# Weight sums by GpSimd, and other shares of the work at a layer boundary

## The chip, the cores and the metric

The kernel runs on one core of a Trainium2 chip. The metric is the device time of one execution in microseconds (us); the median of the runs shown stands for a kernel. PE is TensorE, DVE is VectorE, ACT is ScalarE, POOL is GpSimd, SP is SyncE, whose queue issues most transfers.

## The reference

Two layers over 512 tokens of 1024 channels, in float32: an even layer (pooling mixer and gated mixer) and an odd one (dilated attention and short convolution). Cut to what the change touches:

```python
def even_layer(x, norm_g, w_in, pool_w, pool_scale, ws, bs, w_out):
    h = rmsnorm(x, norm_g)
    z = h @ w_in
    a, g_a, u, v, g_b = jnp.split(...)
    y_a = multiscale_pool(a, pool_w, pool_scale) * jax.nn.silu(g_a)
    y_b = chunk_spatial_gate(u, v, ws, bs) * jax.nn.silu(g_b)
    return x + jnp.concatenate([y_a, y_b], axis=-1) @ w_out

def odd_layer(x, norm_g, w_in, conv_w, w_out):
    h = rmsnorm(x, norm_g)
    z = h @ w_in
    ...
```

## The kernel before

Every product of the float32 data is made of three matmuls of high and low parts (`mm3`), so each tile of weights is loaded by SP as 128x2048 (1 MB), copied into its high part by ScalarE (L92, L226) and subtracted into its low part by VectorE (L93, L227). A `project` takes one such tile for 48 matmuls. The even layer runs, for each of four groups, `mixer_a` (projects a, ga) and `mixer_b` (u, gb), with the two halves of v ahead of groups 0 and 2. Three raw tiles (r...) are used in turn, so SP's queue can load about three projects ahead.

The output projection (`OutProj`, names eo and oo) and the odd layer's value products (`values`, names v0, w0, w1) each use seven products instead of eight, with sums and differences of quarters. Four of the seven factors on the weight side are sums of two or three blocks. There are 28 such sums of 1 MB: 8 for eo, 12 for the values (v), 8 for oo. Before, each is made in DRAM: SP copies one block into the sum's place (`copy_behind`, L190) and GpSimd's queue issues a DMA that adds another block into it (`add_behind`, L196). Block 6 is built on 7 and block 4 on 6, so some of the adding DMAs wait for another to land, and the wait stands in GpSimd's own order of instructions.

At the boundary between the layers the output projection ends in Z (product 4) and Y (product 3). VectorE adds the accumulated halves into the residual stream xt (L331, L336), and `normed` squares both halves of a tile of 128 tokens (L116, ScalarE), forms the reciprocal root with some 128x1 steps on VectorE (L118 to L123; ScalarE's Sqrt, L119), and scales two halves (L126, VectorE) into xb. `to_channels` transposes xb on TensorE (tx, L148), evicts it as hoh (L156, ScalarE) and hol (L157, VectorE) and once more as h32 (L159, ScalarE; the profile calls it h). The tiles of odd number, 1 and 3, come first; product 3 for the first half of the tiles runs ahead of tile 1's transposes, and for the second half behind them. Then v0Z (product 4 of the values) runs, then the transposes of tiles 0 and 2, then v0Y and v0X.

The order on each engine follows from a scheduler with priorities and is fixed in the program.

Of the kernel before, what the change touches and what calls it, by code (L numbers as in the profile page):

```python
# [30 lines left out]
def trunk(ctx, tc, x, w_even, w_eout, pool_w, ws_t, bs, par, g_even, w_v, w_odd, w_oout, g_odd, g_fin, cst, out):  # L31
# [74 lines left out]
        T.matmul(acc, al, bh, start=False, stop=last)  # L106


    def normed(tt, g, name, acc=None, then=None):
        o = sp.tile([P, D], F32, tag="xn", name=name, bufs=3)  # L110
        st = sp.tile([P, 64], F32, tag="st", name="st" + name, bufs=4)
        for h in range(2):
            xs = xt[:, tt, h * S:(h + 1) * S]
            if acc:
                V.tensor_add(xs, acc[h], xs)
            A.activation(o[:, h * S:(h + 1) * S], xs, AF.Square, accum_out=st[:, h:h + 1])  # L116
        ss, m, rt, u = (st[:, i:i + 1] for i in range(2, 6))
        V.tensor_add(ss, st[:, 0:1], st[:, 1:2])  # L118
        A.activation(rt, ss, AF.Sqrt, scale=1.0 / D, bias=eps[:, 0:1])  # L119
        V.tensor_scalar(m, ss, -0.5 / D, -0.5 * EPS, op0=ALU.mult, op1=ALU.add)  # L120
        V.reciprocal(rt, rt)
        V.scalar_tensor_tensor(u, rt, m, rt, op0=ALU.mult, op1=ALU.mult)
        V.scalar_tensor_tensor(u, u, 1.5, rt, op0=ALU.add, op1=ALU.mult)  # L123
        for h in range(2):
            at = slice(h * S, (h + 1) * S)
            V.scalar_tensor_tensor(o[:, at], xt[:, tt, at], u, g[:, at], op0=ALU.mult, op1=ALU.mult)  # L126
            if then:
                then(h, o[:, at])
        return o


# [41 lines left out]

    copies, adds = [], []

    def summed(src, name):
        n = src.shape[1]
        sums = {i: [dp.tile([P, CH], F32, tag=f"{name}{i}{q}", name=f"{name}{i}{q}") for q in range(n)] for i in range(4, 8)}  # L180
        b11, b12, b21, b22 = ([src[i, q] for q in range(n)] for i in range(4))
        for i, first, more in ((7, b12, b22), (5, b11, b12), (6, b11, sums[7]), (4, b21, sums[6])):
            copies.extend((sums[i][q], first[q]) for q in range(n))
            adds.extend((sums[i][q], more[q]) for q in range(n))
# [48 lines left out]


    class OutProj:
        def __init__(self, src, name, yy):
# [4 lines left out]
            self.src = summed(src, name)  # L241

        def form(self, view, n):
            f = ring(f"{self.name}f{n}").rearrange("p (w k t) -> p w k t", w=2, k=KT)
# [22 lines left out]
            self.f1 = self.form(b[0, 0], 1)  # L267
            V.tensor_sub(b[0, 0], b[0, 0], b[0, 1])

        def run(self, gains, half1, half0):  # L270
            with ExitStack() as stack:
                pool = stack.enter_context(tc.tile_pool(name=f"{self.name}w", bufs=1))
                self.chunks = Chunks(pool, 2)
                g = gain(pool, gains, f"g{self.name}")
                self.products(lambda t: half1(t, g), lambda t: half0(t, g))

        def products(self, half1, half0):
# [36 lines left out]
            f4 = self.form(b[1, 1], 4)  # L314
            for t in range(2):
                V.tensor_add(x(2 * t, 0), acc["X", t], x(2 * t, 0))

            both("Y", False, f6, w6)
            w4 = [self.parts(4, q) for q in range(2)]
# [23 lines left out]
    with ExitStack() as ec:  # L343
# [9 lines left out]
        def v_half(c):  # L353
# [17 lines left out]
            if c == 0:  # L371
                load(0, 4)
                to_channels(0, normed(0, ge, "xa0"), hth, htl)
                nc.sync.dma_start(xt[:, 1, :], x[P:2 * P, :])
                o = normed(1, ge, "xa1")
                load(1, 4)
                for tt in range(2, TT):
                    nc.sync.dma_start(xt[:, tt, :], x[tt * P:(tt + 1) * P, :])
                nc.sync.dma_start(pr, par)
                nc.sync.dma_start(wt, ws_t)  # L380
                nc.sync.dma_start(bsb.rearrange("p g t -> p (g t)"), bs.partition_broadcast(P))
                nc.sync.dma_start(cs[:, P:], cst[:, P:])
# [66 lines left out]
        def mixer_b(g, vb):  # L449
# [18 lines left out]
        even_out = OutProj(w_eout, "eo", yy)  # L468
        v_src = [summed(w_v[n:n + 1].rearrange("n b p c -> b n p c"), f"v{n}") for n in range(3)]

        for c in range(2):
            vb = v_half(c)
# [1 line left out]
                mixer_a(g)  # L474
                mixer_b(g, vb)

    o = {}
    odd = []

    def norm1(t, g):  # L480
        o[2 * t + 1] = normed(2 * t + 1, g, f"xb{2 * t + 1}")

    def norm0(t, g):
        if not odd:
            odd.extend(activations("ho"))
            odd.append(ring("h32", F32).rearrange("p (k t) -> p k t", k=KT))
        to_channels(2 * t + 1, o[2 * t + 1], *odd)
        o[2 * t] = normed(2 * t, g, f"xb{2 * t}")

    even_out.run(g_odd, norm1, norm0)  # L490
    hth, htl, h32 = odd


    slopes = [2.0 ** (-8.0 * (n + 1) / (SLOTS * N_DIL)) for n in range(SLOTS * N_DIL)]
    with ExitStack() as oc:
# [4 lines left out]
        def values():  # L500
# [17 lines left out]
            with ExitStack() as vc:  # L518
# [388 lines left out]
```

## Time and profile before

| | us |
|---|---|
| median of 3 runs | 1090.57 (1090.28 to 1090.58) |
| the profiled execution, its own time | 1091.0 |
| its span in the profile | 1089.2 |
| TensorE busy in the span | 1066.2 (98%) |
| VectorE, ScalarE, GpSimd busy | 573.8, 428.4, 191.8 |

The span runs from the first instruction to the last; 1.8 us of the execution's own time lie outside it. Busy time is a sum over the span, without instructions that only issue or wait.

### The profile page before, as it was taken

How to read it: one execution, taken by the hardware profiler on the slowest of the kernel's cores; microseconds unless marked ns; L12 is line 12 of the kernel's file. 1: busy time of each engine (PE TensorE's matmuls, PEld its weight loads, DVE VectorE, ACT ScalarE, POOL GpSimd, SP SyncE). 2: the span in 40 equal slices, each digit the busy share in tenths (PEclk: the TensorE clock that was granted, in tenths of full speed). 3: DMA queues.
4: the chain of work that ended last, by engine and by line, in shares of the span. 5: the costliest groups of instructions: out<-in, count | busy, mean ns of one | idle time of the engine just before them, and what ended most of it. 6: DMA issues, size and time to landing. Idle time of an engine off the chain costs nothing.

```text
span 1089.2 us, 12416 instructions
## 1 busy us (share of the span) xinstructions
PE 1066.2 (98%) x4928; PEld 891.4 (82%) x4928; DVE 573.8 (53%) x708; ACT 428.4 (39%) x583; POOL 191.8 (18%) x501
## 2 busy tenths in 40 slices
PE   6999999999998999999999999999999999999997
PEld 5888888888876888888888888888888888888885
DVE  6343324268969758824453534454444633434986
ACT  6322222326549554424252442434424322223644
POOL 0001030211050200003241442414134011010101
PEclk9999999999998999999999999999999999999999
DMA  9783599499999455663226263544131232223452
GB/s 335 304 326 119 193 265 286 113 245 282 324 272 250 155 193 190 257 270 133 78 78 155 78 155 97 136 116 118 75 113 43 97 116 100 94 102 131 155 193 77
DMA packets 36985, 185.69 MB, mean 170 GB/s; under 512 B 3328, under 2 KB 4480, under 8 KB 22272
## 3 DMA queue, kind: packets, MB, share of 16 engines
q1 hardware_dynamic: 21568, 154.50, 37.9%
q0 software_dynamic: 14784, 29.36, 15.0%
q10 hardware_dynamic: 576, 1.05, 0.3%
q8 instruction: 38, 0.62, 0.2%
q14 instruction: 19, 0.16, 0.0%
HBM read 182.80 MB, written 60.82 MB: 224 GB/s over the span
## 4 chain that ended last, share of the span: by engine, by line
PE 96%; DVE 2%; ACT 1%; DMA 1%; issue 0%; SPq 0%; DVEq 0%
PE q L106 8%; PE q L104 8%; PE q L105 8%; PE v L104 1%; PE v L106 1%; PE v L105 1%; PE gc L106 1%; PE gc L105 1%; PE u L105 1%; PE dx L104 1%; PE dx L106 1%; PE db L106 1%; PE dc L104 1%; PE gc L104 1%; PE dc L106 1%; PE gd L106 1%
## 5 line engine op out<-in xcount | busy, mean ns | idle before, releaser
L104 PE MATMUL q<-hoh,hq 128*128 128x512 f32 x384 | 151.1, 393 | 0.0
L106 PE MATMUL q<-hoh,lq 128*128 128x512 f32 x384 | 149.7, 390 | 0.0
L105 PE MATMUL q<-hol,hq 128*128 128x512 f32 x384 | 149.5, 389 | 0.0
L106 PEld LDWEIGHTS q<-hoh,lq 128*128 128x128 f32 x384 | 72.1, 188 | 15.2
L105 PEld LDWEIGHTS q<-hol,hq 128*128 128x128 f32 x384 | 72.2, 188 | 14.6
L104 PEld LDWEIGHTS q<-hoh,hq 128*128 128x128 f32 x384 | 72.1, 188 | 14.4
L92 ACT ACTIVATE hq<-rq 128x2048 fp32r<-128x2048 f32 x24 | 46.0, 1916 | 86.4 <-PE q L105 72.4
L93 DVE TENSOR_TENSOR lq<-rq,hq 128x2048 fp32r<-128x2048 f32 x24 | 54.8, 2285 | 16.1 <-ACT hq L92 16.1
L658 DVE COPY qk<-q 128x512 f32<-128x512 f32 x24 | 16.6, 690 | 88.3 <-PE q L106 88.3
L660 ACT ACTIVATE qk<-q 128x512 f32<-128x512 f32 x24 | 14.3, 596 | 72.5 <-PE q L106 72.4
L700 ACT ACTIVATE yo<-yo,nm 128x128 f32<-128x128 f32 (+1 forms) x96 | 39.9, 417 | 5.1 <-DVE nm L692 4.7
L464 POOL TENSOR_TENSOR ye<-ye,sggb 128x1024 f32<-128x1024 f32 x3 | 12.0, 4014 | 162.1 <-ACT sggb L409 162.1
L227 DVE TENSOR_TENSOR lw<-rw,hw 128x2048 fp32r<-128x2048 f32 x14 | 32.4, 2319 | 15.3 <-ACT hw L226 15.3
L227 DVE TENSOR_TENSOR loo<-roo,hoo 128x2048 fp32r<-128x2048 f32 x14 | 34.0, 2435 | 11.4 <-ACT hoo L226 11.4
L226 ACT ACTIVATE heo<-reo 128x2048 fp32r<-128x2048 f32 x14 | 26.7, 1916 | 29.5 <-issue 9.2
L226 ACT ACTIVATE hoo<-roo 128x2048 fp32r<-128x2048 f32 x14 | 26.7, 1915 | 28.6 <-DMA roo<-oo 7.8
L227 DVE TENSOR_TENSOR leo<-reo,heo 128x2048 fp32r<-128x2048 f32 x14 | 33.0, 2365 | 9.2 <-ACT heo L226 9.2
L761 POOL TENSOR_TENSOR yo<-yo,at 128x512 f32<-128x512 f32 x8 | 12.3, 1544 | 140.2 <-DVE at L759 140.2
L226 ACT ACTIVATE hw<-rw 128x2048 fp32r<-128x2048 f32 x14 | 26.7, 1910 | 20.1 <-PE w0Y L538 6.0
L724 DVE TENSOR_SCALAR yo<-yo,ff 128x128 f32<-128x128 f32 (+1 forms) x96 | 23.3, 299 | 17.1 <-POOL ff L722 14.2
L790 POOL TENSOR_TENSOR yo<-cv,dc 128x512 f32<-128x512 f32 x6 | 13.2, 2205 | 92.3 <-ACT dc L789 92.3
L759 DVE TENSOR_TENSOR at<-oa,at 128x512 f32<-128x512 f32 x8 | 5.5, 691 | 40.4 <-ACT at L758 40.4
(394 smaller groups left out, 2841.2 us busy)
## 6 DMA issues: line engine op xcount, KB each, us to landing
rq<-in_w_odd SPq DMA_DIRECT2D x24, 1024.0 KB, 4.8
reo<-eo SPq DMA_DIRECT2D x8, 1024.0 KB, 8.0
rw<-v SPq DMA_DIRECT2D x8, 1024.0 KB, 4.8
roo<-oo SPq DMA_DIRECT2D x8, 1024.0 KB, 4.7
reo<-in_w_eout SPq DMA_DIRECT2D x6, 1024.0 KB, 7.7
v<-in_w_v POOLq DMA_DIRECT2D x6, 1024.0 KB, 20.1
v<-v POOLq DMA_DIRECT2D x6, 1024.0 KB, 13.5
rw<-in_w_v SPq DMA_DIRECT2D x6, 1024.0 KB, 4.8
```

Source lines behind the costliest of these rows:

```text
L92: A.activation(hi[:, at], raw[:, at], AF.Copy)
L93: V.tensor_sub(lo[:, at], raw[:, at], hi[:, at].bitcast(F32))
L104: T.matmul(acc, ah, bh, start=first, stop=False)
L105: T.matmul(acc, ah, bl, start=False, stop=False)
L106: T.matmul(acc, al, bh, start=False, stop=last)
L226: A.activation(hi, raw, AF.Copy)
L227: marks["lo"] = V.tensor_sub(lo, raw, hi.bitcast(F32))
L658: V.tensor_copy(to, by)
L660: A.activation(to, by, AF.Copy, scale=HEAD ** -0.5)
L700: A.activation(v, v, AF.Exp, bias=nm[:, g, n:n + 1], accum_out=ls[:, g, n:n + 1])
L724: V.tensor_scalar_mul(v, v, ff[:, g, n:n + 1])
L790: (V if c == 3 else G).tensor_mul(y[4 + c][:, j, :], cv[j][:, 0:S], dc[j][:, 0:S])
```

## The change

Three things change. First, the sums for eo and for the first two of the three value sets (16 MB of the 28) are made on the chip: 16 steps, each of which loads four blocks as one 128x4x512 tile into one half of a ring tile named sums (L232), lets GpSimd do four adds of 128x512 in place (L234), and stores the four results as one transfer (L225). The load of a step and the store of the step before it are issued by SP behind the weight load of a project. The four sums of the third value set are made as before, by a copy and an adding DMA, and these DMAs now stand between the adds. Second, in the first three groups the product of mf and the gate goes from GpSimd to VectorE. Third, at the boundary `normed` is split. The half of a tile that is finished first is squared early (`square`), GpSimd multiplies that half by the gain (L140) and makes two 128x1 steps, and `normed_rest` squares the late half, scales the early half on ScalarE (L147) and the late one on VectorE (L148). For tiles 0 and 2 h32 is made by GpSimd from hoh and hol, and GpSimd makes the first difference of h32 (L638).

```diff
+    def square(pool, tt, h):
+        st = sp.tile([P, 64], F32, tag="st", name=f"stxb{tt}", bufs=4)
+        junk = pool.tile([P, S], F32, tag="sq", name=f"sq{tt}", bufs=2)
+        A.activation(junk, xt[:, tt, h * S:(h + 1) * S], AF.Square, accum_out=st[:, 0:1])
+        G.tensor_scalar(st[:, 1:2], st[:, 0:1], 1.0 / D, EPS, op0=ALU.mult, op1=ALU.add)
+        G.tensor_scalar(st[:, 2:3], st[:, 0:1], -0.5 / D, -0.5 * EPS, op0=ALU.mult, op1=ALU.add)
+        return st
+
+    def normed_rest(tt, h, st, g, name):
...
+        G.tensor_mul(o[:, other], xt[:, tt, other], g[:, other])
+        A.activation(o[:, late], xt[:, tt, late], AF.Square, accum_out=s1)
+        A.activation(rt, s1, AF.Sqrt, scale=1.0 / D, bias=e0)
+        V.tensor_scalar(m, s1, -0.5 / D, m0, op0=ALU.mult, op1=ALU.add)
...
+        A.activation(o[:, other], o[:, other], AF.Copy, scale=u)
+        V.scalar_tensor_tensor(o[:, late], xt[:, tt, late], u, g[:, late], op0=ALU.mult, op1=ALU.mult)
...
             A.activation(dh, bv, AF.Copy)
+            if h32 is not None and tt % 2:
+                A.activation(d32, bv, AF.Copy)
             V.tensor_sub(dl, bv, dh.bitcast(F32))
-            if h32 is not None:
-                A.activation(d32, bv, AF.Copy)
+            if h32 is not None and tt % 2 == 0:
+                G.tensor_add(d32, dh.bitcast(F32), dl.bitcast(F32))
...
+    def sum_behind(load):
+        with tc.issue_after(load.ins):
+            if under_way:
+                dst, t = under_way.pop()
+                nc.sync.dma_start(dst, t)
...
+            src, dst = steps.pop(0)
+            t = pool_sums[0][:, len(steps) % 2]
+            nc.sync.dma_start(t, src)
+        for a, b, c in ((3, 3, 1), (1, 1, 0), (0, 0, 3), (2, 2, 0)):
+            marks["sum"] = G.tensor_add(t[:, a], t[:, b], t[:, c])
+        under_way.append((dst, t))
...
         wh, wl = weights(src, name)
-        copy_behind(marks["load"], 2 if name[0] in "ua" else 1)
+        if name != "a0":
+            sum_behind(marks["load"])
+        copy_behind(marks["load"], 1)
...
-                self.last = G.tensor_sub(x(2 * t + 1, 0), x(2 * t + 1, 0), v[:, t, :])
-            add_behind(self.last, 4)
+                G.tensor_sub(x(2 * t + 1, 0), x(2 * t + 1, 0), v[:, t, :])
+                if early:
+                    early(2 * t + 1, 1)
...
-                add_behind(G.tensor_mul(mf, mf, sg), (0, 4, 12)[g])
+                V.tensor_mul(mf, mf, sg)
+                if g == 2:
+                    add_behind(marks["sum"], 4)
...
-                        V.tensor_sub(hb[0, 1], hb[0, 1], hb[1, 1])
+                        G.tensor_sub(hb[0, 1], hb[0, 1], hb[1, 1])
```

The order on GpSimd from the start of the even layer to the output projection, before (L464 is the product with the gate, L196 an adding DMA, xt the residual stream):

```order
L464 TENSOR_TENSOR ye<-ye,sggb_873 128x1024
L196 DMA eo_94<-in_w_eout 512x512
L196 DMA eo_95<-in_w_eout 512x512
L196 DMA eo_90<-in_w_eout 512x512
L196 DMA eo_91<-in_w_eout 512x512
L464 TENSOR_TENSOR ye<-ye,sggb_1285 128x1024
L196 DMA eo_92<-eo_94 512x512
L196 DMA eo_93<-eo_95 512x512
L196 DMA eo_88<-eo_92 512x512
L196 DMA eo_89<-eo_93 512x512
```

And after (L234 is an add of a step, L246 an adding DMA):

```order
L234 TENSOR_TENSOR sums<-sums 128x512 x52
L246 DMA v_95<-in_w_v 512x512
L246 DMA v_93<-in_w_v 512x512
L246 DMA v_94<-v_95 512x512
L246 DMA v_92<-v_94 512x512
L234 TENSOR_TENSOR sums<-sums 128x512 x12
L355 TENSOR_TENSOR xt<-xt,eos_1796 128x512 x2
```

The adding DMAs for eo and for two value sets are gone; the four that are left stand after the adds of the thirteenth step, ahead of the adds of steps 14 to 16.

The order on SP at the end of the even layer, before (L190 is a copy, ra to rgb the weights of a project, reo those of the output projection):

```order
L91 DMA ra_1366<-in_w_even 128x2048
L190 DMA v_106<-in_w_v 16x16384
L190 DMA v_104<-in_w_v 16x16384
L91 DMA rga_1443<-in_w_even 128x2048
L419 DMA pwr_1358<-in_pool_w 128x2x256
L91 DMA ru_1513<-in_w_even 128x2048
L91 DMA rgb_1592<-in_w_even 128x2048
```

And after (L232 loads a step, L225 stores one; the store in the second row is step 13's, the one ahead of ru is step 14's):

```order
L91 DMA ra_1406<-in_w_even 128x2048
L225 DMA v_91<-sums 128x4x512
L232 DMA sums<-in_w_v 128x4x512
L91 DMA rga_1487<-in_w_even 128x2048
L232 DMA sums<-in_w_v 128x4x512
L475 DMA pwr_1398<-in_pool_w 128x2x256
L225 DMA v_91<-sums 128x4x512
L91 DMA ru_1563<-in_w_even 128x2048
L225 DMA v_91<-sums 128x4x512
L232 DMA sums<-in_w_v 128x4x512
L91 DMA rgb_1648<-in_w_even 128x2048
L225 DMA v_91<-sums 128x4x512
```

The load of ru now stands behind the store of step 14, which needs the fourteenth group of GpSimd's adds.

The order on VectorE at the boundary from the addition of tile 0's late half, before (stxb and xb belong to the norm, lv to the values' weights, hol to the evictions of tile 1 and then tile 3):

```order
L126 SCALAR_TENSOR_TENSOR xb_2093<-xt,stxb_2094,geo 128x512 x2
L157 TENSOR_TENSOR hol<-tx_2133,hoh 128x512
L157 TENSOR_TENSOR hol<-tx_2141,hoh 128x512
L118 TENSOR_TENSOR stxb_2150<-stxb_2150 128x1
L120 TENSOR_SCALAR stxb_2150<-stxb_2150 128x1
L121 RECIPROCAL stxb_2150<-stxb_2150 128x1
L122 SCALAR_TENSOR_TENSOR stxb_2150<-stxb_2150 128x1
L123 SCALAR_TENSOR_TENSOR stxb_2150<-stxb_2150 128x1
L126 SCALAR_TENSOR_TENSOR xb_2149<-xt,stxb_2150,geo 128x512 x2
L227 TENSOR_TENSOR lv_2232<-rv_2229,hv_2231 128x2048
```

And after:

```order
L391 TENSOR_TENSOR xt<-eoY_1869,xt 128x512
L143 TENSOR_SCALAR stxb_2001<-stxb_2001 128x1
L144 RECIPROCAL stxb_2001<-stxb_2001 128x1
L145 SCALAR_TENSOR_TENSOR stxb_2001<-stxb_2001 128x1
L146 SCALAR_TENSOR_TENSOR stxb_2001<-stxb_2001 128x1
L148 SCALAR_TENSOR_TENSOR xb_2218<-xt,stxb_2001,geo 128x512
L279 TENSOR_TENSOR lv_2297<-rv_2294,hv_2296 128x2048
L179 TENSOR_TENSOR hol<-tx_2202,hoh 128x512
L179 TENSOR_TENSOR hol<-tx_2210,hoh 128x512
L391 TENSOR_TENSOR xt<-eoY_1882,xt 128x512
```

Tile 1's two evictions into hol now stand behind tile 0's norm and behind a weight difference lv; before they stood ahead of both.

## Rows read from the trace of the kernel before

**Rows 1.** Windows, whole program: length, busy per engine, granted clock, transfer share, GB/s.

```profile
12.00:300.00 288.00, 287.59 (x1304) 238.25 (x1304) 147.85 (x137) 104.59 (x105) 28.66 (x22) 1.00 0.82 255
300.00:355.00 55.00, 48.58 (x210) 39.52 (x209) 44.02 (x55) 38.94 (x50) 15.28 (x11) 0.94 0.95 255
355.00:1050.00 695.00, 695.00 (x3268) 584.92 (x3267) 352.51 (x462) 259.25 (x389) 142.59 (x460) 1.00 0.40 131
```

**Rows 2.** Waits of PE at the boundary, 300 to 360: total us, times, longest us.

```profile
PE tx L148 <- DVE xb L126: 4.3, 2, 2.2
PE v0Z L536 <- ACT hoh L156: 0.9, 1, 0.9
PE v0Y L538 <- DVE vf L232: 0.8, 1, 0.8
PE v0Z L538 <- DVE hol L157: 0.4, 1, 0.4
```

**Rows 3.** A window at the boundary, columns as in rows 1.

```profile
348.00:350.00 2.00, 1.85 (x4) 1.49 (x5) 2.00 (x4) 2.00 (x3) 0.00 (x0) 0.50 1.04 349
```

**Rows 4.** PE's timeline: start, duration, instruction, [idle before, releaser].

```profile
227.91 0.48 PE L104 MATMUL u<-heh,hu 128*128 128x512 f32 x1
...
325.71 0.55 PE L148 MATMUL tx<-cs,xb 128*128 128x128 f32 x3 [2.21 <-DVE xb L126]
...
354.65 0.40 PE L536 MATMUL v0X<-hv,hoh 128*128 128x512 f32 x1
```

**Rows 5.** GpSimd's timeline, columns as in rows 4.

```profile
89.06 4.01 POOL L464 TENSOR_TENSOR ye<-ye,sggb 128x1024 f32<-128x1024 f32 x1 [69.32 <-ACT sggb L409]
...
310.82 1.30 POOL L325 TENSOR_TENSOR xt<-xt,eov 128x512 f32<-128x512 f32 x1
312.06 2.01 POOL L196 DMA_DIRECT2D v<-in_w_v  x2
...
338.70 1.04 POOL L196 DMA_DIRECT2D v<-v  x1 [13.63 <-DMA v<-v]
```

**Rows 6.** VectorE's timeline, columns as in rows 4.

```profile
88.53 2.29 DVE L93 TENSOR_TENSOR lga<-rga,hga 128x2048 fp32r<-128x2048 f32 x1 [9.75 <-ACT hga L92]
...
310.95 3.31 DVE L227 TENSOR_TENSOR leo<-reo,heo 128x2048 fp32r<-128x2048 f32 x1 [3.17 <-ACT heo L226]
...
318.37 2.28 DVE L227 TENSOR_TENSOR leo<-reo,heo 128x2048 fp32r<-128x2048 f32 x1
...
329.20 2.02 DVE L157 TENSOR_TENSOR hol<-tx,hoh 128x512 fp32r<-128x512 f32 x2
```

**Rows 7.** A window of the even layer, columns as in rows 1.

```profile
30.00:250.00 220.00, 219.98 (x1005) 183.11 (x1004) 89.97 (x80) 62.46 (x59) 24.57 (x15) 1.00 0.73 229
```

**Rows 8.** SyncE's queue: start of each issue, duration.

```profile
19.66 0.52 SPq L91 DMA_DIRECT2D ru<-in_w_even  x1
...
150.05 0.33 SPq L91 DMA_DIRECT2D rgb<-in_w_even  x1
...
182.45 0.34 SPq L91 DMA_DIRECT2D ru<-in_w_even  x1
```

**Rows 9.** Transfers: KB each, median us to landing; first 12 to 60, then 160 to 210.

```profile
ru<-in_w_even SPq DMA_DIRECT2D x1, 1024.0 KB, 16.3
...
rga<-in_w_even SPq DMA_DIRECT2D x1, 1024.0 KB, 9.5
...
rgb<-in_w_even SPq DMA_DIRECT2D x1, 1024.0 KB, 4.7
```

**Rows 10.** ScalarE's timeline, columns as in rows 4.

```profile
215.35 1.92 ACT L92 ACTIVATE hu<-ru 128x2048 fp32r<-128x2048 f32 x1 [4.66 <-PE a L105]
...
314.21 1.92 ACT L226 ACTIVATE hv<-rv 128x2048 fp32r<-128x2048 f32 x1 [3.29 <-DMA rv<-v]
...
322.64 1.28 ACT L119 ACT_TABLE_LOAD   x1
...
326.63 2.00 ACT L156 ACTIVATE hoh<-tx 128x512 fp32r<-128x512 f32 x2
```

More of the change, by code (lines that the diff above doesn't have):

```diff
@@ L106, in mm3, with normed @@
         T.matmul(acc, al, bh, start=False, stop=last)
-    def normed(tt, g, name, acc=None, then=None):
+    def normed(tt, g, name):
         o = sp.tile([P, D], F32, tag="xn", name=name, bufs=3)
@@ L126, in normed @@
             V.scalar_tensor_tensor(o[:, at], xt[:, tt, at], u, g[:, at], op0=ALU.mult, op1=ALU.mult)
-            if then:
-                then(h, o[:, at])
+        return o
+    def square(pool, tt, h):
[6 more added lines that the diff above has]
+    def normed_rest(tt, h, st, g, name):
+        o = sp.tile([P, D], F32, tag="xn", name=name, bufs=3)
+        s1, e0, m0, rt, m, u = (st[:, i:i + 1] for i in (3, 1, 2, 4, 5, 6))
+        late, other = (slice(n * S, (n + 1) * S) for n in (h, 1 - h))
+        G.tensor_mul(o[:, other], xt[:, tt, other], g[:, other])
+        A.activation(o[:, late], xt[:, tt, late], AF.Square, accum_out=s1)
+        A.activation(rt, s1, AF.Sqrt, scale=1.0 / D, bias=e0)
+        V.tensor_scalar(m, s1, -0.5 / D, m0, op0=ALU.mult, op1=ALU.add)
+        V.reciprocal(rt, rt)
+        V.scalar_tensor_tensor(u, rt, m, rt, op0=ALU.mult, op1=ALU.mult)
+        V.scalar_tensor_tensor(u, u, 1.5, rt, op0=ALU.add, op1=ALU.mult)
+        A.activation(o[:, other], o[:, other], AF.Copy, scale=u)
+        V.scalar_tensor_tensor(o[:, late], xt[:, tt, late], u, g[:, late], op0=ALU.mult, op1=ALU.mult)
         return o
@@ L172, in tick, with summed @@
                 item[1]()
-    copies, adds = [], []
-    def summed(src, name):
+    copies, adds, steps, under_way = [], [], [], []
+    pool_sums = [None]
+    def summed(src, name, on_chip):
         n = src.shape[1]
-        sums = {i: [dp.tile([P, CH], F32, tag=f"{name}{i}{q}", name=f"{name}{i}{q}") for q in range(n)] for i in range(4, 8)}
         b11, b12, b21, b22 = ([src[i, q] for q in range(n)] for i in range(4))
-        for i, first, more in ((7, b12, b22), (5, b11, b12), (6, b11, sums[7]), (4, b21, sums[6])):
-            copies.extend((sums[i][q], first[q]) for q in range(n))
-            adds.extend((sums[i][q], more[q]) for q in range(n))
-        return {1: b11, 2: b21, 3: b22, **sums}
+        if on_chip:
+            both = [dp.tile([4, P, CH], F32, tag=f"{name}{q}", name=f"{name}{q}") for q in range(n)]
+            for q in range(n):
+                for i in range(4):
+                    at = slice(i * S, (i + 1) * S)
+                    steps.append((src[:, q, :, at].rearrange("b p c -> p b c"), both[q][:, :, at].rearrange("b p c -> p b c")))
+            sums = {m: [both[q][i] for q in range(n)] for i, m in enumerate((6, 5, 4, 7))}
+        else:
+            sums = {i: [dp.tile([P, CH], F32, tag=f"{name}{i}{q}", name=f"{name}{i}{q}") for q in range(n)]
+                    for i in range(4, 8)}
+            for i, first, more in ((7, b12, b22), (5, b11, b12), (6, b11, sums[7]), (4, b21, sums[6])):
+                copies.extend((sums[i][q], first[q]) for q in range(n))
+                adds.extend((sums[i][q], more[q]) for q in range(n))
+        return {1: b11, 2: b21, 3: b22, **sums}
+    def sum_behind(load):
[3 more added lines that the diff above has]
+                nc.sync.dma_start(dst, t)
+            if not steps:
+                return
+            if pool_sums[0] is None:
+                pool_sums[0] = ring("sums", F32).rearrange("p (s b c) -> p s b c", s=2, b=4)
+            src, dst = steps.pop(0)
[4 more added lines that the diff above has]
+        under_way.append((dst, t))
     def copy_behind(load, n):
@@ L240, in __init__ @@
             self.bank = {}
-            self.src = summed(src, name)
+            self.src = summed(src, name, on_chip)
         def form(self, view, n):
@@ L268, in prepare, with run @@
             V.tensor_sub(b[0, 0], b[0, 0], b[0, 1])
-        def run(self, gains, half1, half0):
+        def run(self, gains, half1, half0, early=None):
             with ExitStack() as stack:
@@ L274, in run, with products @@
                 g = gain(pool, gains, f"g{self.name}")
-                self.products(lambda t: half1(t, g), lambda t: half0(t, g))
-        def products(self, half1, half0):
+                self.products(lambda t: half1(t, g), lambda t: half0(t, g), early and (lambda tt, h: early(pool, tt, h)))
+        def products(self, half1, half0, early):
             b, nm, acc = self.block, self.name, self.bank
@@ L316, in products @@
                 V.tensor_add(x(2 * t, 0), acc["X", t], x(2 * t, 0))
+                if early:
+                    early(2 * t, 0)
             both("Y", False, f6, w6)
@@ L324, in products @@
                 G.tensor_add(x(2 * t + 1, 1), x(2 * t + 1, 1), v[:, t, :])
-                self.last = G.tensor_sub(x(2 * t + 1, 0), x(2 * t + 1, 0), v[:, t, :])
-            add_behind(self.last, 4)
+                G.tensor_sub(x(2 * t + 1, 0), x(2 * t + 1, 0), v[:, t, :])
+                if early:
+                    early(2 * t + 1, 1)
             both("Z", False, f4, w4, True)
@@ L398, in v_half @@
                     load(kh)
+                    sum_behind(marks["load"])
                     for t in range(TT):
@@ L463, in mixer_b @@
                 sg = gate(w_even[7 + 4 * g], f"gb{g}")
-                add_behind(G.tensor_mul(mf, mf, sg), (0, 4, 12)[g])
+                V.tensor_mul(mf, mf, sg)
+                if g == 2:
+                    add_behind(marks["sum"], 4)
             else:
                 sg = gate(w_even[7 + 4 * g], f"gb{g}", lambda j, t: V.tensor_mul(mf[:, j, :], mf[:, j, :], t))
-        even_out = OutProj(w_eout, "eo", yy)
-        v_src = [summed(w_v[n:n + 1].rearrange("n b p c -> b n p c"), f"v{n}") for n in range(3)]
+        even_out = OutProj(w_eout, "eo", yy, True)
+        v_src = [summed(w_v[n:n + 1].rearrange("n b p c -> b n p c"), f"v{n}", n < 2) for n in range(3)]
         for c in range(2):
@@ L475, in trunk, with early @@
                 mixer_b(g, vb)
-    o = {}
+    o, st = {}, {}
     odd = []
+    def early(pool, tt, h):
+        st[tt] = square(pool, tt, h)
     def norm1(t, g):
-        o[2 * t + 1] = normed(2 * t + 1, g, f"xb{2 * t + 1}")
+        o[2 * t + 1] = normed_rest(2 * t + 1, 0, st[2 * t + 1], g, f"xb{2 * t + 1}")
     def norm0(t, g):
@@ L487, in norm0 @@
         to_channels(2 * t + 1, o[2 * t + 1], *odd)
-        o[2 * t] = normed(2 * t, g, f"xb{2 * t}")
-    even_out.run(g_odd, norm1, norm0)
+        o[2 * t] = normed_rest(2 * t, 1, st[2 * t], g, f"xb{2 * t}")
+    even_out.run(g_odd, norm1, norm0, early)
     hth, htl, h32 = odd
```

6 lines of the change are left out of this document (2 added, 4 removed).

## The prediction

> **What bounds the kernel now.** I read the windows over the whole program first: TensorE works 287.59 of 288 us in the even layer and all of 355 to 1050; between them, at the layer boundary, it works 48.58 of 55 us and at a mean granted clock of 0.94 [rows 1]. So the kernel is bound by TensorE, and only the boundary has something to give: 6.4 us of idle time, and 48.58 x 0.06 = 2.9 us from the clock, 9.3 us in all. The waits of TensorE say where: twice for xb (4.3 us in all, the longest 2.2), 0.9 for hoh, 0.4 for hol, 0.8 for the form vf [rows 2]. One of the windows behind them stands at 0.50, the lower of the two levels (1.2 of 2.4 GHz), with TensorE busy before and behind [rows 3]. Even layer and odd layer can only lose. A change of under 0.2% (2.2 us) can't be told from none by a measurement of this kernel.
>
> **The change, part by part: the sums.** Of the 28 copies with their adding DMAs 16 go. TensorE waits for no transfer in the rows [rows 2], so taking them away gives nothing; what covers them is that each sum is due long after it is made. What comes in is a chain with a due time. A step is a load, four adds on GpSimd, a store, and SP issues the store ahead of the next project's weights, so SP stops where GpSimd is late. I follow it to the one place where it matters, the load of the last u weights (ru), behind the store of step 14.
>
> TensorE takes these weights at 227.91 [rows 4]. A split needs ScalarE 1.92 us [rows 10] and VectorE 2.29 [rows 6], together 4.2. A transfer of 1 MB lands after 4.7 alone and 9.5 among others [rows 9]; I take 8, since each project now has a load and a store beside its weights. So ru must leave SP by 227.9 - 4.2 - 8 = 215.7; before, it left at 182.45 [rows 8], 33 us earlier.
>
> When does step 14's store leave? A GpSimd add of 128x512 takes 1.30 us when alone [rows 5], so four take 5.2. But the two engines get in each other's way: a GpSimd product of 128x1024 took 4.01 us from 89.06, where VectorE's 128x2048 difference ran from 88.53 to 90.82; without these first 1.76 us it would be 2.25 [rows 5, 6]. And VectorE's difference of 310.95 took 3.31 instead of 2.28 beside a GpSimd op that ended at 312.12 [rows 5, 6]. VectorE is busy 89.97 of 220 us of the even layer, 41% [rows 7], a part of it with an input from PSUM, where I see no such delay. So four adds cost from 5.2 to 5.2 / 0.59 = 8.8; I take 7. The Trainium skill ("SBUF — State Buffer", "Who interferes with whom") says that a VectorE instruction with two SBUF inputs and a GpSimd instruction that reads SBUF exclude each other for a whole instruction; the two pairs of rows agree.
>
> Two steps share the ring tile and overlap: store, load (with its landing), four adds, four adds. A pair costs a landing of 4.7 to 9.5 [rows 9], two groups of adds (10.4 to 17.6) and some 0.6 of issues: 15.7 to 27.7, and I take 8 + 14 + 0.6 = 22.6. The first step's load stands just ahead of ru, which leaves at 19.66 [rows 8] and lands 16.3 later among the first loads [rows 9]; so it lands at about 32 and its adds end near 38. Six pairs on, the thirteenth step ends at 38 + 136 = 174. It can't end before its load does, which stands behind gb's weights at 150.05 [rows 8]: 150.4 + 4.7 + 5.2 = 160. With the high ends it ends at 38 + 166 = 204.
>
> Behind the thirteenth step GpSimd issues the four adding DMAs that are left. The third waits for the first to land, the fourth for the third. The same four took from 312.06 to 338.70 + 1.04, 27.7 us, before [rows 5]; two lone landings would be some 23. Then the adds of step 14 (7), the store, and ru. Middle: 174 + 27.7 + 7 + 0.6 = 209.3 against 215.7, so TensorE doesn't wait, with 6 us to spare. Cost nil; the cover is those 6 us, and past them each us is lost on TensorE. Best: 160 + 23 + 5.2 + 0.6 = 189. Worst: 204 + 34 + 8.8 + 0.6 = 247, some 32 us late, if everything is slow at once.
>
> The Trainium skill ("GPSIMD Engine Reference", "Engine selection") puts elementwise work on VectorE, since GpSimd takes about twice as long; its table has 4.5 us for 2048 columns, so an estimate by that page is 1.1 us for 512. By that, the four adds would take 4.5 us and the middle would have a few us more to spare; the row, 1.30, goes.
>
> The product with the gate, on VectorE three times, is no cost: GpSimd's 4.01 us become some 1.2 of an engine that is 41% busy [rows 5, 7].
>
> **The boundary.** Squares taken early take 0.63 us of ScalarE and one half of VectorE's scaling (0.7 of 1.4) out of the chain from the last addition to xb. I count the chain anew by the order of each engine.
>
> First stall. Before, GpSimd ended its two pairs of xt updates at 312.12 [rows 5], ahead of most of VectorE's difference [rows 6]. After, a gain product (1.30) and two small steps stand between the pairs, so the second pair begins after VectorE's difference has begun, waits for its end (312.8) and ends its first half at 314.2. ScalarE's early square of tile 3 waits for that, and stands ahead of hv, which moves from 314.21 [rows 10] to 314.9; VectorE's lv and leo then meet GpSimd's other products (1.3 each). The last leo, which began at 318.37 and took 2.28 [rows 6], ends at about 322.6 instead of 320.65. TensorE, which needs it at 320.3, waits 2.2. From there the chain is an addition 0.7, a square 0.8, the table load 1.28 [rows 10], Sqrt 0.3, four small steps 0.8, the scaling 0.75: the transposes of tile 1 begin at 326.9 instead of 325.71 [rows 4]: +1.2.
>
> Second stall. 32 matmuls and the transposes further, at about 334.8, TensorE needs tile 1's hol. VectorE has it behind lv, which waits for ScalarE's hv, which stands behind four evictions (from 328.4, two took 2.00 at 326.63 [rows 10], with an overlap: 0.92 each), a square 0.8 and a Sqrt 0.3: hv from 333.2 to 335.1, lv to 337.4, and two hol of 1.0 each [rows 6] to 339.4. TensorE waits 4.6 where it waited 0.9 + 0.4 [rows 2]: +3.3. Before, hol ran at 329.20 [rows 6].
>
> Third stall. Tile 2's scaled half waits on ScalarE behind vf and another hv: 348.1 against 345.4, 2.8, where it was 2.1 + 0.8: nil.
>
> So TensorE idles 2.2 + 1.7 + 4.6 + 2.8 = 11.3 us at the boundary, against 6.4. If the clock stays up, the 2.9 of before come back: 11.3 - 9.3 = +2.0. Followed along the program instead, v0X begins at 354.6 against 354.65 [rows 4]: 0. The idle time before v0Z is longer than that which stood ahead of the lower level before, so I expect some of it again, 0 to 2.9. My value is +2 in the middle of 0 and 4.9.
>
> **Sum.** 1091.0 of the profiled execution + 0 (sums) + 2 (boundary) = 1093.0. That execution is 0.4 above the median, so 1092.6 for the median.
>
> **The rivals.**
> Slower by more: GpSimd's queue makes SP late, and with it ru. Its point is step 13's end: past 174 + 6.4 = 180.4 TensorE waits. For it: the adds and VectorE's differences collide, and DMA is 73% busy in the even layer already [rows 7]. Against it: the raw tiles let SP run 33 us ahead. Its time: 2 to 14 us above the forecast, 1095 to 1107. The Trainium skill ("GPSIMD Engine Reference", "Engine selection", above) speaks for it.
> Faster: GpSimd comes ahead of VectorE's difference at 311, so that leo ends at 320.65 as before. Then all three stalls move up by about 2 us, and with the clock up the boundary ends 2 to 4 us earlier: 1087 to 1089. For it: two engines that wait for each other alternate, and a us decides which is first. Against it: GpSimd begins its pair only at 311.1, with VectorE at 310.5.
> No effect: hol is hidden by an earlier hv and the clock stays up: 1090 to 1092.
>
> **How the numbers follow.** Forecast, boundary +0.5 to +4.9 with no stall in the even layer: 0.36, a third of it within 0.2%. Late ru: 0.26, all slower. Faster boundary: 0.22. No effect: 0.16. So faster 0.22, within 0.2% 0.12 + 0.16 = 0.28, slower 0.50. The likeliest one's own range is 1091 to 1095.5. To leave out no more than 2 in 10, the range reaches down into the faster case to 1088 and up through most of the late case to 1102.
>
> **What would show it.** Right: ru leaves SP before 215.7 and TensorE has no wait from 30 to 300; the waits for hol at v0Z are 3 to 5 us in all; hv at about 314.9; leo ends past 322. Wrong: TensorE's wait for hu or lu near 228, with GpSimd's adding DMAs ending past 205; or tile 1's transposes ahead of 325.7 and a clock of 1.00 up to 355. A wait at another project would mean that the stores hold SP from early on. The prediction is wrong as a whole if GpSimd and VectorE don't collide at the adds, since both the spare time and the first stall rest on that.

## The result and the profile after

The changed kernel takes 1102.16 us (median of four runs, 1101.03 to 1102.62), against 1090.57 before: a ratio of 1.0097, 95% interval 1.0083 to 1.0111 (it is taken over the runs, a fourth run of before at 1093.42 us included; the two medians alone give 1.0106). It is slower, as forecast, but by 11.6 us where 2 were forecast. Its profiled execution took 1102.19 us with a span of 1100.4, 11.2 us above that of before.

The windows answer to [rows 1] (length, busy time of PE, PEld, DVE, ACT and POOL, granted clock, DMA share, GB/s):

```profile
12.00:300.00 288.00, 287.43 (x1302) 238.18 (x1301) 166.40 (x142) 102.81 (x109) 111.97 (x75) 1.00 0.79 271
300.00:355.00 55.00, 46.18 (x199) 37.70 (x198) 38.53 (x42) 37.47 (x46) 21.98 (x18) 0.91 0.42 153
355.00:370.00 15.00, 9.59 (x41) 8.71 (x40) 11.38 (x9) 7.43 (x9) 8.45 (x4) 0.89 0.16 65
```

The even layer is as full as before, 287.43 of 288 us. GpSimd's busy time in it has gone from 28.66 to 111.97 us without costing TensorE anything in this execution. The loss stands at the boundary: 46.18 of 55 us instead of 48.58, and 9.59 of the next 15, where there was no gap before; the clock is at 0.91 and 0.89. From 370 to 1060 TensorE is busy all of the time.

TensorE's waits answer to [rows 2] (total us, times, longest):

```profile
PE v0X L597 <- ACT s1n L620: 5.4, 1, 5.4
PE v0Z L599 <- DVE hol L179: 4.1, 1, 4.1
PE eoY L313 <- DVE leo L279: 2.9, 1, 2.9
PE tx L168 <- ACT xb L147: 1.7, 1, 1.7
```

One more, ahead of the first transposes of the program, varies between 8.6 and 10.5 us in the profiles of this study, whatever the kernel; it was 8.9 in that of before and 10.3 here. So 1.3 us of the 11.2 are no work of the change: output product 4 (eoZ) begins at 308.19 instead of 306.89. By the start of v0X the distance has grown to 3.7 us (358.35 instead of 354.65, [rows 4]), so the stalls that the prediction followed cost 2.4 us net. Then comes the largest wait, 5.4 us at v0X, which the prediction does not have. The clock falls behind it: nine matmuls from 369.56 take 4.03 us, the nine behind them 2.16, so that is some 1.9 more. By the next products (w0Z, 393.9 instead of 382.7) the distance is the whole 11.2.

### The profile page after: what moved, and what is told of

Its sections match the earlier page's. It is cut to its first block, busy times and chain, and to the rows that moved or that the text cites. A ratio compares the mean times of both kernels' runs of the same rounds, so it can differ in the third digit from the quotient of the medians.

```text
span 1100.4 us, 12490 instructions
## 1 busy us (share of the span) xinstructions
PE 1068.0 (97%) x4928; PEld 892.6 (81%) x4928; DVE 592.3 (54%) x702; ACT 426.5 (39%) x583; POOL 290.2 (26%) x563
## 4 chain that ended last, share of the span: by engine, by line
PE 93%; ACT 2%; issue 1%; POOL 1%; DVE 1%; DMA 1%; SPq 0%; DVEq 0%; POOLq 0%; ACTq 0%
PE q L106 8%; PE q L105 8%; PE q L104 8%; PE v L104 1%; PE v L106 1%; PE v L105 1%; PE gc L105 1%; PE gc L106 1%; PE dx L106 1%; PE dc L106 1%; PE u L106 1%; PE db L106 1%; PE gc L104 1%; PE u L105 1%; PE gd L106 1%; PE gb L106 1%
## 5 line engine op out<-in xcount | busy, mean ns | idle before, releaser
L234 POOL TENSOR_TENSOR sums<-sums 128x512 f32<-128x512 f32 x64 | 100.2, 1569 | 79.5 <-DMA sums<-in_w_eout 50.7
L822 POOL TENSOR_TENSOR yo<-yo,at 128x512 f32<-128x512 f32 x8 | 12.3, 1543 | 140.1 <-DVE at L820 140.1
```

Source lines behind the costliest of these rows:

```text
L234: marks["sum"] = G.tensor_add(t[:, a], t[:, b], t[:, c])
```

## The experiments

Each is told against the kernel before on its own chip, by the ratio of the times, and against the changed kernel by the medians. The bracketed term is the 95% interval. The kernel before has a median of 1092.32 us beside the runs with the sums alone, the h32 copies back, the difference back and the early squares alone, and of 1091.10 beside the others, so differences of medians between runs can be off by 1 to 2 us; where it matters the difference of the ratios stands beside them.

**The sums alone.** The boundary of before, with the sums by GpSimd:

```diff
...
-    even_out.run(g_odd, norm1, norm0, early)
+    even_out.run(g_odd, norm1, norm0)
...
-        o[2 * t + 1] = normed_rest(2 * t + 1, 0, st[2 * t + 1], g, f"xb{2 * t + 1}")
+        o[2 * t + 1] = normed(2 * t + 1, g, f"xb{2 * t + 1}")
...
-                        G.tensor_sub(hb[0, 1], hb[0, 1], hb[1, 1])
+                        V.tensor_sub(hb[0, 1], hb[0, 1], hb[1, 1])
```

> The changed kernel with the boundary of before: sums by GpSimd in the even layer, norm, scaling and copies at the boundary as before. Boundary theory (the whole loss of 11.6 us stands between 305 and 375 us): 1090 to 1092.5, TensorE with under 0.5 us of waits between 30 and 300. Rival, the sums cost something (the first transposes waited 10.3 us in the changed kernel and 8.9 before, and everything up to 305 us is 1.3 us late): 1091.5 to 1093, with that 1.3 us at the start again. Rival, the sums slow the output projection or the values as well: 1095 or more.

Measured: 1090.44 us, ratio 0.9979 [0.9968, 0.9990]. So the whole loss comes from the boundary's part, and the sums give some 2 us. None of the expectations had that gain. ScalarE's timeline shows where it comes from (start, duration, [idle before, releaser]):

```profile
313.68 1.92 ACT L276 ACTIVATE hv<-rv 128x2048 fp32r<-128x2048 f32 x1 [0.26 <-DMA rv<-v]
```

Before, ScalarE waited 3.29 us for the same transfer of the values' weights [rows 10]; it landed in 8.2 us (8.6 is the median of two), now in 4.8. ScalarE takes its work in order, so the output projection's last split stood behind that wait. The other side of the sums shows in TensorE's waits:

```profile
PE mx L105 <- DVE lpl L100: 0.8, 1, 0.8
...
PE tx L168 <- DVE xb L124: 0.5, 1, 0.5
```

Of the two waits for xb, 4.3 us in all [rows 2], the first is gone and tile 2's is 0.5. A new one of 0.8 stands in the even layer, where under 0.5 was expected: a VectorE difference (lpl) came late there, and the section on the prediction shows behind what.

**Fewer adding DMAs.** The kernel before, without the last five adding DMAs of the values (five additions of blocks are left out):

```diff
             for dst, part in adds[:n]:
+                left[0] -= 1
+                if left[0] < skip[0]:
+                    continue
                 G.dma_start(dst, part, accum_op=ALU.add, max_dma_last_dim=2048)
```

> The kernel before, without its last five adding DMAs of the values' sums (those that run from 300 us on; five additions of weight blocks are left out). Theory (before, these transfers made the values' weights land late, 8.6 us against 4.8 with the sums made on the chip, ScalarE waited 3.3 us for them ahead of the output projection's last split, and TensorE was late by it): they land in about 5 us, ScalarE's wait is under 1 us, TensorE's wait for the odd tiles' xb falls from 2.2 to under 1, and the time is 1.5 to 4 us below the kernel before. Rival (what helped in the run with sums alone is that GpSimd's queue is free): with no gain, within 1 us.

Measured: 1088.37 us, ratio 0.9967 [0.9955, 0.9979]. ScalarE's row and TensorE's wait:

```profile
311.08 1.92 ACT L230 ACTIVATE hv<-rv 128x2048 fp32r<-128x2048 f32 x1 [0.38 <-DMA rv<-v]
...
PE tx L148 <- DVE xb L126: 0.5, 1, 0.5
```

The load lands in 4.8 us, hv begins 3.9 us after eoZ (307.15 here) instead of 7.3, the wait for the odd tiles' xb is gone (the 0.5 shown is tile 2's), and the time falls as the theory has it. The edit frees GpSimd's queue as well, so the rival is not excluded by the time alone; but GpSimd's first pair of updates moved by only 0.5 us against eoZ (306.84 here, 307.07 before), which is not the 3.4 of hv.

**The h32 copies back.** The changed kernel, with ScalarE making all four tiles' copies:

```diff
             A.activation(dh, bv, AF.Copy)
-            if h32 is not None and tt % 2:
-                A.activation(d32, bv, AF.Copy)
             V.tensor_sub(dl, bv, dh.bitcast(F32))
-            if h32 is not None and tt % 2 == 0:
-                G.tensor_add(d32, dh.bitcast(F32), dl.bitcast(F32))
+            if h32 is not None:
+                A.activation(d32, bv, AF.Copy)
```

> The changed kernel with the h32 copies of tiles 0 and 2 on ScalarE again, as before; all else as changed. Theory (GpSimd's four copies of 2.13 us each hold the difference for form 6, the form stands ahead of the eviction of the first half of v0X on ScalarE, and TensorE waits for that): the 5.4 us wait at v0X goes, and with it the lower clock behind it (about 3 us), but ScalarE gets four evictions of 0.9 us back: 1093 to 1096. Rival (the chain is held by VectorE's differences and not by the copies): the wait stays above 3 us, 1098 to 1101.

Measured: 1096.51 us, ratio 1.0034 [1.0020, 1.0048]; 5.7 us below the changed kernel (6.9 by the ratios), just past the theory's upper end. TensorE's waits:

```profile
PE tx L168 <- ACT xb L147: 3.9, 1, 3.9
...
PE tx L168 <- DVE xb L148: 1.6, 1, 1.6
...
PE v0Z L597 <- DVE hol L177: 0.4, 1, 0.4
```

The wait at v0X is gone. So is most of that for hol (0.4 is left), since the scheduler put tile 1's hol ahead of tile 0's norm and of lv again; so this run undoes two things at once, and the run with hol first, below, tells them apart. Waits for xb are longer in their place.

**And the difference of h32 back.** The same, and:

```diff
-                        G.tensor_sub(hb[0, 1], hb[0, 1], hb[1, 1])
+                        V.tensor_sub(hb[0, 1], hb[0, 1], hb[1, 1])
```

> As the run before it, and the first difference of h32 on VectorE again. Theory (GpSimd's 2.85 us op and VectorE's weight difference beside it, 3.82 instead of 2.28, hold each other): form 5 and tile 2's transposes come some 1.5 to 2.5 us earlier, so 0.5 to 2 us below the run before it. Rival (that wait is set by ScalarE's order alone): within 0.5 us of it.

Measured: 1094.75 us, ratio 1.0018 [1.0009, 1.0028]; 1.8 us below the run before it, as the theory had it. The wait for tile 2's xb falls from 3.9 to 2.1; one of 1.0 at v0X comes in.

**Early squares alone.** In `normed_rest` GpSimd's product and ScalarE's scaling go as well:

```diff
-        G.tensor_mul(o[:, other], xt[:, tt, other], g[:, other])
...
-        A.activation(o[:, other], o[:, other], AF.Copy, scale=u)
+        V.scalar_tensor_tensor(o[:, other], xt[:, tt, other], u, g[:, other], op0=ALU.mult, op1=ALU.mult)
```

> Of the boundary's changes only the early squares are left (with their two 128x1 steps on GpSimd); gain products, scaling, h32 copies and the difference of h32 are as before. Theory (GpSimd's gain product between its two pairs of updates of the residual delays tile 3's square, hv and with them the last weight difference, 2.9 us of TensorE): that wait is under 1 us, 1090 to 1093. Rival (the two small steps are enough, since one of them took 2.12 us beside a VectorE difference): the wait stays above 2 us and the time is 1 us or less below the run before it.

Measured: 1089.71 us, ratio 0.9972 [0.9960, 0.9984]. TensorE has no wait for leo, as the theory says, and the time is 5.0 us below the run with GpSimd's products, a little under the range. ScalarE's scaling went with the products, so this run doesn't tell the two apart; the run with the gain product late, below, does.

**The order of hol.** The changed kernel, with tile 1's hol ahead of the weight difference and of the first of tile 0's norm steps:

```diff
+        with (tc.issue_after(marks["hol", 1].ins) if tt == 0 else ExitStack()):
-        V.tensor_scalar(m, s1, -0.5 / D, m0, op0=ALU.mult, op1=ALU.add)
+            V.tensor_scalar(m, s1, -0.5 / D, m0, op0=ALU.mult, op1=ALU.add)
...
+            with (tc.issue_after(marks["hol", 1].ins) if name == "v05" else ExitStack()):
-            marks["lo"] = V.tensor_sub(lo, raw, hi.bitcast(F32))
+                marks["lo"] = V.tensor_sub(lo, raw, hi.bitcast(F32))
```

> The changed kernel, with tile 1's two hol evictions put ahead of tile 0's norm steps and of the weight difference lv on VectorE. Theory (TensorE's 4.1 us before v0Z's first hol, and the lower clock of 340 to 346 behind it, come from that order): the wait falls under 2 us, the clock of 340 to 346 is above 0.9, and the time falls 3 to 6 us, to 1096 to 1099. Rival (the time is set further on, by GpSimd's h32 copies, so that an earlier v0Z only waits longer at v0X): v0Z's wait falls, v0X's grows by as much, and the time is within 1.5 us of the changed kernel.

Measured: 1102.51 us, ratio 1.0102 [1.0085, 1.0119]: no change. The rival holds in the time, if not in its details. TensorE's waits:

```profile
PE v0X L599 <- ACT s1n L622: 4.5, 1, 4.5
PE tx L169 <- ACT xb L148: 4.1, 2, 2.6
...
PE v0Z L601 <- DVE hol L180: 0.8, 1, 0.8
```

GpSimd's copies:

```profile
351.81 10.99 POOL L182 TENSOR_TENSOR h<-hoh,hol 128x512 f32<-128x512 f32 x4 [5.92 <-DVE hol L180]
```

The wait for hol falls from 4.1 to 0.8 (and 1.0 for hoh), that for xb from ScalarE grows from 1.7 to 4.1, and v0X still waits, 4.5. The clock, which the theory had above 0.9 from 340 to 346, falls to 0.50 at 344. What is spared at one place is waited for at the next: the four copies begin 3.1 us earlier than in the changed kernel (351.81 instead of 354.93) but take 10.99 us instead of 8.52, so they end only 0.7 us earlier, at 362.80.

**The gain product late.** The changed kernel, with GpSimd's product and small steps for tile 1 behind both pairs of updates:

```diff
...
+        if tt == 3:
+            with tc.issue_after(marks["pair"].ins):
+                marks["rest"]()
...
+        with (tc.issue_after(marks["pair"].ins) if tt == 1 else ExitStack()):
-        G.tensor_mul(o[:, other], xt[:, tt, other], g[:, other])
+            G.tensor_mul(o[:, other], xt[:, tt, other], g[:, other])
```

> The changed kernel, with GpSimd's gain product and small steps for tile 1 behind both pairs of updates of the residual. Theory (between the pairs they delay tile 3's square, hv and the last weight difference): the second pair begins before 311.5, hv before 315 (both against a Z product that begins at 308.2), and TensorE's wait of 2.9 us for leo is under 1 us; the time falls by 1 to 3 us if that is not taken back at v0X. Rival (it is VectorE's difference beside the pair, whichever comes first): the wait stays above 2 us.

Measured: 1098.36 us, ratio 1.0063 [1.0048, 1.0078]; 3.8 us below the changed kernel (3.7 by the ratios), more than expected. GpSimd's timeline and ScalarE's hv:

```profile
310.00 1.29 POOL L387 TENSOR_TENSOR xt<-xt,eov 128x512 f32<-128x512 f32 x1 [5.02 <-DVE eov L386]
...
312.51 1.30 POOL L387 TENSOR_TENSOR xt<-xt,eov 128x512 f32<-128x512 f32 x1
...
315.15 2.12 POOL L133 TENSOR_SCALAR stxb<-stxb 128x1 f32<-128x1 f32 x1
...
314.47 1.90 ACT L287 ACTIVATE hv<-rv 128x2048 fp32r<-128x2048 f32 x1
```

The pairs follow each other, the second from 312.51 with eoZ at 310.11 (2.40 after it), where in the changed kernel it began 7.43 after eoZ. hv begins 4.4 us after eoZ instead of 9.4, and the wait for leo is gone. The waits for hol (4.2) and at v0X (5.4) are as they were, but what they wait for has moved up with the chain (the copies begin at 351.37), so here the time does fall.

**Squares of tiles 0 and 2 only.** As the run of the squares, with `normed` for tiles 1 and 3:

```diff
-                if early:
-                    early(2 * t + 1, 1)
...
-        o[2 * t + 1] = normed_rest(2 * t + 1, 0, st[2 * t + 1], g, f"xb{2 * t + 1}")
+        o[2 * t + 1] = normed(2 * t + 1, g, f"xb{2 * t + 1}")
```

> Sums by GpSimd, and of the boundary's changes only the early squares of tiles 0 and 2, whose half is finished long before; tiles 1 and 3 as before, scaling, copies and differences on the engines of before. Theory (tile 3's early square is what delays hv, since it waits for GpSimd's second pair; tiles 0 and 2 only gain): no wait for leo, the first xb wait under 1 us, 1087.5 to 1089.5 against 1089.7 with all four early. Rival (the early squares of tiles 1 and 3 shorten the first chain by more than they delay): 1090 or more.

Measured: 1089.62 us, ratio 0.9988 [0.9979, 0.9997]. There is no wait for leo and no first wait for xb, as the theory says. By the medians this equals the run with four early squares; by the ratios it is no better. So the run doesn't tell the two apart, and that tile 3's early square delays hv is not shown by it.

**All of it, mended.** The three edits together: gain product late, h32 copies on ScalarE, difference on VectorE.

```diff
...
+        with (tc.issue_after(marks["pair"].ins) if tt == 1 else ExitStack()):
+            G.tensor_mul(o[:, other], xt[:, tt, other], g[:, other])
...
+                A.activation(d32, bv, AF.Copy)
...
+                        V.tensor_sub(hb[0, 1], hb[0, 1], hb[1, 1])
```

> All of the change, with GpSimd's gain product and small steps for tile 1 behind both pairs, the h32 copies on ScalarE and the difference of h32 on VectorE. If the three losses add up (place of the gain product 3.8 us, copies 5.7, difference 1.8, all measured apart): 1102.2 - 11.3 = 1090.9, so 1090 to 1092. If the gain product and ScalarE's scaling cost in any place (tile 1's second half is scaled on ScalarE behind tile 3's square): 1092.5 to 1094, and the wait for xb from ScalarE stays above 1.5 us.

Measured: 1089.63 us, ratio 0.9993 [0.9977, 1.0008]. The three losses add up, and a little more; 12.5 us have come off the changed kernel by the medians, 11.3 by the ratios (one of the ten runs took 1097.41). TensorE's waits:

```profile
PE tx L177 <- ACT xb L156: 2.1, 1, 2.1
PE v0Z L604 <- ACT hoh L185: 1.3, 1, 1.3
PE v0Y L606 <- DVE vf L291: 1.0, 1, 1.0
PE v0X L604 <- ACT s1n L627: 1.0, 1, 1.0
PE tx L177 <- DVE xb L157: 0.9, 1, 0.9
```

With one of 0.4 for hol they sum to 6.7 us, about as before [rows 2]. ScalarE's scaling is still waited for, 2.1 us, as the second expectation had it, but the time is not that one's.

**The first half scaled first.** The early squares alone, with the two scalings in the order of the halves:

```diff
+        for n in range(2):
+            at = slice(n * S, (n + 1) * S)
+            V.scalar_tensor_tensor(o[:, at], xt[:, tt, at], u, g[:, at], op0=ALU.mult, op1=ALU.mult)
```

> As the run with the early squares alone, with VectorE scaling the first half of a tile first (there the late half came second, and TensorE waited 1.85 us for tile 1's first half). Theory (that order costs one scaling of 0.7 us of the first wait): the wait is 1.0 to 1.3 us, the time 0.3 to 1 us below 1089.7, a ratio to the kernel before of 0.996 to 0.998. Rival (the time is given back at the next wait): no change, 0.997 to 0.999.

Measured: 1089.32 us, ratio 0.9986 [0.9975, 0.9997]. Its profile has no first wait for xb at all (the one left is 2.0 at tile 2), but a wait of 0.8 in the even layer. The ratio is the rival's; the median, 0.4 us below 1089.7, would fit the theory, so the time doesn't decide. The fastest versions, sums with or without early squares, stand at ratios of 0.997 to 0.999, and the intervals don't rank them.

## Why the prediction went as it did

**Right in this profile, and only just: the sums don't cost TensorE anything in the even layer.** GpSimd's timeline around the thirteenth step, and SP's queue behind it:

```profile
158.15 12.68 POOL L234 TENSOR_TENSOR sums<-sums 128x512 f32<-128x512 f32 x8 [8.12 <-DMA sums<-in_w_v]
170.78 2.31 POOL L246 DMA_DIRECT2D v<-in_w_v  x2
...
201.76 1.03 POOL L246 DMA_DIRECT2D v<-v  x1 [12.63 <-DMA v<-v]
202.41 14.08 POOL L234 TENSOR_TENSOR sums<-sums 128x512 f32<-128x512 f32 x8
```

```profile
208.25 0.37 SPq L225 DMA_DIRECT2D v<-sums  x1
208.68 0.50 SPq L91 DMA_DIRECT2D ru<-in_w_even  x1
```

Steps 12 and 13 end at 170.8 (174 was said). The adding DMAs hold GpSimd until 202.4, 32 us instead of 27.7. The store of step 14 leaves at 208.25 (209.3 was said), and ru behind it 7 us ahead of its due 215.7. Four adds take 5.4 alone and 7.2 beside VectorE, and two groups took 12.7 to 14.1; 5.2 and 7 were said. That the sum comes out within 1.1 us is in part luck: the steps ended 3 us early and the DMAs took 4 us longer.

The late ru, which had a chance of 0.26, did not come here, but in other runs with the same even layer it did, in small. In ten profiles with the sums, ru leaves at 208 to 209.5 in three and at 215.1 to 216.7 in seven, where the thirteenth step ended at 174 to 176: the spare time is used up. From the run with hol first (SP, ScalarE and TensorE):

```profile
216.11 0.50 SPq L91 DMA_DIRECT2D ru<-in_w_even  x1
...
223.43 1.92 ACT L92 ACTIVATE hu<-ru 128x2048 fp32r<-128x2048 f32 x1 [12.35 <-DMA ru<-in_w_even]
...
255.41 0.50 PE L316 MATMUL eoX<-heo,eof 128*128 128x512 f32 x1 [1.15 <-DVE eof L286]
```

TensorE doesn't wait for ru's split itself. But VectorE's work behind that split comes late (lu begins at 225.38, in the changed kernel at 218.61), and with it a form (eof, a sum or difference of quarters: 253.06 instead of 247.40) that the output projection needs. In the six profiles in which ru left at 215.5 or later TensorE waits 1.2 to 1.4 us for eof (four) or 0.8 for another difference (lpl, two); in the four others there is no such wait. So the due time of 215.7 was well placed, and "cost nil" holds for some executions only.

**Wrong: "taking them away gives nothing".** TensorE's waits named no transfer, and I stopped there. But [rows 10] has ScalarE waiting 3.29 us for one, ahead of a split that TensorE needs. The runs with the sums alone and with fewer adding DMAs show what it was worth: 1.9 and 2.7 us by the medians, 2.3 and 3.6 by the ratios.

**Right with the sizes off: the first stall.** The second pair came behind the gain product and the small steps, and these ran into VectorE's difference. GpSimd's timeline, then VectorE's:

```profile
309.31 1.28 POOL L378 TENSOR_TENSOR xt<-xt,eov 128x512 f32<-128x512 f32 x1 [5.02 <-DVE eov L377]
...
313.17 0.19 POOL L132 TENSOR_SCALAR stxb<-stxb 128x1 f32<-128x1 f32 x1
313.42 2.12 POOL L133 TENSOR_SCALAR stxb<-stxb 128x1 f32<-128x1 f32 x1
315.62 1.29 POOL L378 TENSOR_TENSOR xt<-xt,eov 128x512 f32<-128x512 f32 x1
...
354.93 8.52 POOL L181 TENSOR_TENSOR h<-hoh,hol 128x512 f32<-128x512 f32 x4 [8.52 <-DVE hol L179]
```

```profile
313.19 2.30 DVE L279 TENSOR_TENSOR leo<-reo,heo 128x2048 fp32r<-128x2048 f32 x1 [3.37 <-ACT heo L278]
...
337.38 2.29 DVE L279 TENSOR_TENSOR lv<-rv,hv 128x2048 fp32r<-128x2048 f32 x1 [0.41 <-ACT hv L278]
339.59 2.01 DVE L179 TENSOR_TENSOR hol<-tx,hoh 128x512 fp32r<-128x512 f32 x2
...
361.37 3.15 DVE L643 TENSOR_TENSOR h<-h 128x1024 f32<-128x1024 f32 x1 [3.49 <-POOL h L181]
```

The small step of 313.42 took 2.12 us: it too waited for VectorE's difference to end, at 315.49. So the pair begins at 315.62, behind that difference, as was said. What was mis-sized is the difference's own start: 313.19, or 311.9 without the late start, where the forecast had 310.5. It follows a square and a split on ScalarE that wait for GpSimd's first pair, and that pair began at 309.31, behind VectorE's eov, 0.9 us later than before (late start taken off). So hv begins at 317.58 (314.9 was said; 316.3 without the late start), and TensorE waits 2.9 for leo, not 2.2. The run with the product late takes all of it away.

**Right, and without weight: the second and third stall.** The wait for hol was 4.1 (4.6 was said), that for tile 2's xb 1.7 (2.8 was said). lv ran from 337.38 and hol from 339.59 behind it, by the order that the prediction read. But the run with hol first shows that, as long as GpSimd's copies set what follows, mending this order moves the wait and doesn't shorten the time.

**Luck, twice.** Up to v0X the boundary lost 2.4 us, and +2 was said, but not by the sum that was said. TensorE's waits from eoZ to v0X come to 8.8 us (2.91, 4.14 and 1.74), 2.4 more than the 6.4 of before, not 11.3: the 1.7 for tile 1's xb did not come, since TensorE came to these transposes late itself (329.49), and tile 2's wait was smaller. And the 2.9 us of the clock, which the sum takes back, did not come back: TensorE is busy for 41.4 us of this stretch in both profiles, and windows at 0.50 stand behind two of its waits (below). The two errors cancel. The time as a whole, 1102.16, stands at the upper end of the stated range, 1102. That end was drawn for a late ru; the time got there by another way, the one that follows.

**The step that failed: the account ended at the first matmul of v0X.** "v0X begins at 354.6 against 354.65" stops there, and what stands behind it I didn't follow. VectorE's difference (361.37 above) waits for GpSimd's four copies into h32, 8.52 us from 354.93; before, ScalarE made them at about 1.0 each. The difference is released at 361.37 and then takes 3.15 us instead of 1.23, past the end of the last copy at 363.45. No term of the sum has these copies. ScalarE's timeline shows the rest of the chain:

```profile
317.58 1.90 ACT L278 ACTIVATE hv<-rv 128x2048 fp32r<-128x2048 f32 x1
...
364.56 1.17 ACT L283 ACTIVATE vf<-h 128x1024 fp32r<-128x1024 f32 x1 [7.57 <-DVE h L643]
...
366.07 1.16 ACT L283 ACTIVATE vf<-h 128x1024 fp32r<-128x1024 f32 x1
367.10 1.93 ACT L278 ACTIVATE hv<-rv 128x2048 fp32r<-128x2048 f32 x1
368.90 0.61 ACT L620 ACTIVATE s1n<-v0X 128x512 f32<-128x512 f32 x1
```

Two forms (vf) and a split stand ahead of the eviction of v0X's first half (s1n, 368.90) in ScalarE's order. The next product adds to the same accumulators in PSUM, so TensorE can't go on before that: 5.4 us from 364. Then the clock, by windows:

```profile
326.00:328.00 2.00, 2.00 (x6) 1.52 (x5) 0.45 (x2) 1.97 (x5) 0.00 (x0) 0.50 1.00 410
340.00:344.00 4.00, 2.34 (x6) 1.90 (x7) 3.67 (x5) 4.00 (x6) 0.44 (x1) 0.50 0.74 262
368.00:372.00 4.00, 2.44 (x6) 2.00 (x7) 4.00 (x4) 4.00 (x5) 0.00 (x0) 0.50 0.00 0
```

It is at the lower level, 0.50 of full speed, behind each of the three long waits, as it was behind the idle time of before [rows 3]. The forecast's bound for the clock, 2.9 us, was made for one such stretch. The boundary's part costs 11.7 us by the medians (the changed kernel against the sums alone; 12.9 by the ratios). The copies' run takes away 5.7 of it (6.9 by the ratios; the order of hol is included, which alone gives none), the product's 3.8 (3.7), the difference's 1.8 (1.7): 11.3 in all (12.3), and the mended version has all of them, 12.5 (11.3).

## What to carry to other kernels

When work moves to an engine that is idle, price each moved instruction and follow its reader to the end of the stage; the engine's small share of busy time says nothing about the instruction that is waited for. An in-order queue turns a wait into a wait of everything behind it: here a transfer delayed a split behind it on ScalarE, and copies on GpSimd delayed an eviction two forms later. When stalls follow each other, one that is mended alone may only move: the wait for hol fell by 3.3 us and the time not at all, since the copies behind it ended when they had ended. The first stall, mended alone, gave 3.8 us, since the chain behind it moved up. So ask, before mending one, what sets the start of the next. And a spare time of a few us is a matter of the execution: look at more than one profile.

## What the runs showed of the hardware

GpSimd's 128x512 copy into h32 took 2.13 us, against 1.30 for its adds between contiguous tiles; VectorE worked during a part of it only (idle from 357.9 to 361.37). The copy reads and writes every fourth element of its tiles, which those adds do not; whether that makes the difference was not tried.

GpSimd's 128x1 step is as exposed to VectorE's differences as a large one: 0.19 us alone, 2.12 beside one of 2.30. The Trainium skill ("SBUF — State Buffer", "Who interferes with whom") says that the second of the two to issue is blocked until the first is done, whatever its size; the row agrees.

With adding DMAs of 1 MB under way, two plain loads of 1 MB (rv) landed in 8.2 and 8.9 us; in the run with fewer adding DMAs the same two took 4.9 and 4.7.
